# Dense routing weights of an expert layer: one-hot products on TensorE, or 4-byte adds into DRAM by indirect DMA

## The chip, the cores and the metric

The kernel runs on one core of one Trainium2 chip. The metric is the device time of one execution in microseconds (us). Five engines work side by side, each through its own instruction queue in order: PE (TensorE, matrix products), DVE (VectorE), ACT (ScalarE), POOL (GpSimd) and SP (SyncE, which here only issues DMAs). Sixteen DMA engines move data; DMAs are issued from SP, ACT and POOL, and indirect ones, which take their row addresses from a table, from POOL only.

## The reference, cut to what matters

The program is a two-layer backbone (512 latent tokens, 256 context tokens, width 1024). Each layer ends in a product-key expert layer, and the change lies there:

```
q = (hb @ w_q).reshape(n, PEER_HEADS, 2, PEER_DK_HALF)
s = jnp.einsum('nhpk,pek->nhpe', q, keys)
v_top, i_top = lax.top_k(s, PEER_TOPK)
...
e = i1 * N_KEYS + i2
g = jax.nn.softmax(sc.astype(jnp.float32), axis=-1).astype(hb.dtype)
a = jax.nn.gelu(jnp.einsum('nhkd,nd->nhk', u_tab[e], hb)) * g
return jnp.einsum('nhk,nhkd->nd', a, v_tab[e])
```

Each token picks 16 experts in each of 8 heads, 128 slots in all, out of 16,384 experts. An expert is one row of `u_tab` and one of `v_tab`. Two heads of a token may pick the same expert; within a head the 16 are different.

## The kernel before, in words

The latent tokens are four blocks of 128. Block 3 is done sparsely: for each of its 128 slots an indirect DMA gathers the 128 tokens' rows of `u_tab`, DVE takes the dot product (line L907), and the same is done with `v_tab` (L925). Blocks 0 to 2 (384 tokens) are done densely: for each group of 128 experts (an "s block", 128 of them) PE computes all 384 x 128 products `s`, ACT applies the gelu, DVE multiplies by a table of weights that is zero where a token did not pick an expert, and PE adds the product with the 128 rows of `v_tab` to accumulators (L1160).

The function `peer_lat` runs this once per layer in two stages.

1. *Routing stage.* `routing` computes the top-16 lists on DVE, first for block 3 and then for 0, 1 and 2. For a dense block `use` calls `weights_dense`, which builds the table of weights: for four tokens at a time DVE makes two one-hot arrays (L1072, L1075), PE multiplies them (L1079), ACT copies the result (L1081), and one SP DMA per 32 tokens writes 2 MB to the DRAM tensor `gd` (L1083). Between these steps s blocks are computed ahead of need and stored in the DRAM tensor `sp`: 76 in the first layer, 80 in the second.
2. *Dense stage.* `dense` goes over all 128 s blocks. It reads the weights from `gd` (tile `gr`, L1125) and the stored s blocks from `sp` (tile `gsr`), computes those that were not stored, multiplies, splits into a high and a low part, and accumulates. Three blocks are prepared ahead (`AHEAD`).

The order of the instructions on each engine is fixed when the program is built. `Background` objects hold work that is woven in: `tick(us)` is called after a piece of foreground work with its assumed length, and a background object issues as many steps as its rate allows (`rows_bg` the gathers, `s_bg` the s blocks). In `dense` the remaining gathers are spread evenly over the loop. In the first layer the gathers for the context tokens (`gat<-in_peer_v,ev`, with a PE product at L1020) also run in the routing stage. All POOL DMAs use eight semaphores in turn, so that an indirect DMA waits for the landing of the one eight places ahead of it.

Of the kernel before, what the change touches and what calls it, by code (L numbers as in the profile page):

```python
# [11 lines left out]
F32 = mybir.dt.float32  # L12
# [10 lines left out]
SEQ = 512  # L23
# [30 lines left out]
LAG = 3  # L54
COST_T = (2.0, 4.0)
GB = 5
UB, ULAG, VLAG = 3, 2, 1
GTB, VRB, GRB, GSB = 2, 2, 2, 2
AB, AHEAD = 3, 3


def build(nc, tc, I, out):
# [118 lines left out]

    rows_bg, s_bg, ada_bg, conv_bg = (Background() for _ in range(4))

    def tick(us):
        if not any(bg.busy for bg in (rows_bg, s_bg, ada_bg, conv_bg)):
            for bg in (rows_bg, s_bg, ada_bg, conv_bg):
                bg.tick(us)
# [23 lines left out]
    iota = const("iota", [128, 128])  # L211
    rowstart = const("rowstart", [128, 16])
    ones = mk(pc, [128, 128], F32, "ones")
    V.memset(ones, 1.0)
# [828 lines left out]

    def weights_dense(i12, gw, b, gd):


        ps = psum("sm")
        PE.transpose(ps[:, :128], i12[:, 0, :], ident)
        PE.transpose(ps[:, 128:256], i12[:, 1, :], ident)
        PE.transpose(ps[:, 256:384], gw, ident)  # L1050
        it = mk(ph[1], [128, 4, 128], F32, "itT", 1)
        V.tensor_copy(it[:, 0, :], ps[:, :128])
        V.tensor_copy(it[:, 3, :], ps[:, 256:384])
        ei = mk(ph[1], [128, 2, 128], I32, "ik")
        V.tensor_copy(ei[:, 1, :], ps[:, 128:256])
        V.tensor_scalar(ei[:, 0, :], ei[:, 1, :], 4, None, op0=ALU.logical_shift_right)
        V.tensor_scalar(ei[:, 1, :], ei[:, 1, :], 15, None, op0=ALU.bitwise_and)
        V.tensor_copy(it[:, 1:3, :], ei)
        i128 = iota.unsqueeze(1).to_broadcast([128, 4, 128])
        for tq in range(4):  # L1060
            T32 = slice(32 * tq, 32 * tq + 32)
            bc = lambda i, n: it[:, i, T32].unsqueeze(2).to_broadcast([128, 32, n])
            o8 = mk(ph[1], [128, 32, 8], F32, "o8", 1)
            V.tensor_tensor(o8, iota[:, :8].unsqueeze(1).to_broadcast([128, 32, 8]), bc(1, 8), ALU.is_equal)
            V.tensor_tensor(o8, o8, bc(3, 8), ALU.mult)
            o16 = mk(ph[1], [128, 32, 16], F32, "o16", 1)
            V.tensor_tensor(o16, iota[:, :16].unsqueeze(1).to_broadcast([128, 32, 16]), bc(2, 16), ALU.is_equal)
            gt = mk(ph[1], [128, 128, 32], F32, "gt", GTB)
            for t4 in range(8):
                t = slice(4 * t4, 4 * t4 + 4)  # L1070
                o1 = mk(pt, [128, 4, 128], F32, "rstd")
                V.tensor_tensor(o1, i128, it[:, 0, 32 * tq + 4 * t4:32 * tq + 4 * t4 + 4].unsqueeze(2)  # L1072
                                .to_broadcast([128, 4, 128]), ALU.is_equal)
                o2 = mk(pt, [128, 4, 8, 16], F32, "tA")
                V.tensor_tensor(o2, o8[:, t, :].unsqueeze(3).to_broadcast([128, 4, 8, 16]),  # L1075
                                o16[:, t, :].unsqueeze(2).to_broadcast([128, 4, 8, 16]), ALU.mult)
                ps = psum("sm")
                for i in range(4):
# [27 lines left out]
    def dense(l, h, gd, sp, nsp, nb, x, mod):  # L1106
# [13 lines left out]
        def prepare(gi, ei, held={}):  # L1120

            eb = 4 * gi + ei
            if ei == 0:
                held["g"] = gt = mk(ph[1], [128, 4 * nb, 4, 32], F32, "gr", GRB)
                nc.sync.dma_start(gt.rearrange("p b i t -> p b (i t)"),  # L1125
                                  gd.rearrange("b p x -> p b x")[:, 0:4 * nb, 128 * gi:128 * gi + 128])
            if gi < nsp // 4:
# [7 lines left out]
            g3 = gs.rearrange("p (b t) -> p b t", t=32)  # L1135
            V.tensor_tensor(g3, g3, held["g"][:, :, ei, :], ALU.mult)
            ah = mk(ph[1], [128, T], F32R, "ah", AB)
# [43 lines left out]
    def peer_lat(l, C, mod, first=()):  # L1181
# [3 lines left out]
        with psum_pool(s=2):  # L1185
            with psum_pool(**banks), spool("sp", 1) as sp_pool[0]:
                for v in first:
                    g = rows_bg.add(v, 64, V_COST)
                h = norm_mod(xl[0], SEQ, mod, 0, C["norm2_g"], 3)
                gd = mk(pd, [4 * ND, 128, 128 * 32], F32, "gd")  # L1190
# [11 lines left out]
                s_bg.rate, rows_bg.rate = 0.0, rate  # L1202
# [85 lines left out]
    with psum_pool(mm=3, sm=3, acc=2):  # L1288
# [3 lines left out]
        with spool("cxa", 1) as cxa:  # L1292
# [3 lines left out]
            ag = [third(0, g, mod) for g in range(3)]  # L1296
            ada_bg.finish(ag[0])
            mixer_consts(0, C, cm)
            use_bufs(cx, cx, CTX)
# [48 lines left out]
            s_bg.finish()  # L1348
            ada_bg.finish()
            after[0] = None  # L1350
            cx_cm.__exit__(None, None, None)
# [28 lines left out]
    with psum_pool(mm=3, sm=3, acc=2):  # L1380
# [8 lines left out]
        with spool("zx", 1) as zx:  # L1389
# [4 lines left out]
            with spool("ym", 1) as ym:  # L1394
# [6 lines left out]
                with spool("mp", 1) as mp:  # L1401
                    proj = mlstm_proj(1, C, hl, SEQ, True, mp)
                    rows_bg.finish()
                    for i in range(4):
                        add_ctx(xc, i, ond[i], mod_c)
                    close_right(pg_cm)
                    side[0] = "right"
                    use_bufs(zx, None, CTX)
# [8 lines left out]
        cm_cm.__exit__(None, None, None)  # L1417
        px = lat_tail(1, yp, mod)
    pg_cm, pg[0] = right_pool("pg")
    peer_lat(1, C, mod)  # L1420
# [14 lines left out]
def shape_constants():  # L1435
# [17 lines left out]
    c["iota"] = np.tile(np.arange(128, dtype=f), (128, 1))  # L1453
    c["rowstart"] = np.tile(np.array([min(v, 42) for v in STARTS] + [0] * 8, f), (128, 1))
    n_freq = D // 4
# [77 lines left out]
```

## Time and profile before

| | us |
|---|---|
| three runs, median | 4629.89 |
| lowest, highest | 4601.46, 4631.63 |
| the profiled execution | 4608.01 |
| its span, first to last instruction | 4606.2 |

Over the span PE is busy 92%, DVE 72%, ACT 35% and POOL 28%; the 16 DMA engines move 1187 MB, a mean of 258 GB/s. These shares are means over unlike stages. The stretches that matter here are the routing and the dense stage of either layer: about 1337 to 1855 and 1855 to 2610 us in the first, 3392 to 3852 and 3852 to 4580 us in the second.

### The profile page before, as it was taken

The page shows a single profiled execution, that of the slowest core. Times are in us where ns is not written, and L with a number is a line of the kernel's source. Part 1 is how long each engine was busy: PE and PEld are TensorE (multiplying, and loading weights), DVE is VectorE, ACT ScalarE, POOL GpSimd, SP SyncE. Part 2 cuts the span into 40 slices and gives each one's busy share as a digit, 9 for nine tenths or more (in the row PEclk, how much of TensorE's full clock was granted, in tenths as well). Part 3 has the DMA queues.
Part 4 walks back from the last instruction along what each step waited for, and adds up shares of the span by engine and source line. Part 5 has one row for each costly group of instructions (what it writes and reads, how often), then busy time and mean ns, then how long its engine had stood idle before and what let it go on. Part 6 is the DMA issues. An engine that isn't in the chain of part 4 may idle for free.

```text
span 4606.2 us, 61297 instructions
## 1 busy us (share of the span) xinstructions
PE 4250.9 (92%) x22364; PEld 3462.3 (75%) x22364; DVE 3322.1 (72%) x6764; ACT 1631.4 (35%) x2316; POOL 1294.3 (28%) x1061
## 2 busy tenths in 40 slices
PE   7899759987999999999999888999999999999998
PEld 4695545665667799788888764677789998888887
DVE  4754877866578497777777775365699997777775
ACT  4441222323224355333333321243335554333333
POOL 0000345653233341333334344200012322233231
PEclk9999868998999999999999999979999999999999
DMA  8556768986577896999989787512248889899984
GB/s 286 188 153 223 257 211 312 339 296 202 184 260 250 309 347 239 343 332 326 325 316 335 246 284 253 193 56 73 88 138 298 315 295 319 308 313 306 318 311 161
DMA packets 417342, 1187.42 MB, mean 258 GB/s; under 512 B 39440, under 2 KB 142608, under 8 KB 413968
## 3 DMA queue, kind: packets, MB, share of 16 engines
q1 hardware_dynamic: 260992, 631.52, 40.1%
q0 software_dynamic: 150928, 549.52, 33.6%
q8 instruction: 176, 2.88, 0.2%
q10 hardware_dynamic: 5120, 2.47, 0.2%
q14 instruction: 126, 1.03, 0.1%
HBM read 1092.40 MB, written 90.96 MB: 257 GB/s over the span
## 4 chain that ended last, share of the span: by engine, by line
PE 41%; issue 22%; DMA 14%; DVE 10%; POOL 6%; ACT 2%; ACTq 0%; POOLq 0%; DVEq 0%; SPq 0%
PE mm L312 13%; PE s L312 11%; PE acc L1160 9%; POOL gat L876 4%; DMA gsr<-sp 3%; DMA gat<-in_peer_v,ev 3%; DMA vr<-in_peer_v 3%; POOL ug L876 2%; DMA ug<-in_peer_u,hu 2%; PE sm L1079 2%; DMA gat<-in_peer_v,eu 2%; DVE wl L293 1%; PE mm L778 1%; DMA gat<-in_peer_u,eu 1%; DVE vl L293 1%
## 5 line engine op out<-in xcount | busy, mean ns | idle before, releaser
L292 ACT CAST wh<-wr 128x1024 fp32r<-128x1024 f32 x498 | 521.7, 1048 | 1197.8 <-PE mm L312 688.3
L293 DVE TENSOR_TENSOR wl<-wr,wh 128x1024 fp32r<-128x1024 f32 x498 | 606.8, 1219 | 345.1 <-ACT wh L292 339.9
L312 PE MATMUL s<-hh,wh 128*128 128x384 f32 x2048 | 703.1, 343 | 3.0 <-ACT gs L1103 3.0
L312 PE MATMUL s<-hh,wl 128*128 128x384 f32 x2048 | 695.6, 340 | 4.7 <-DVE wl L293 4.7
L312 PE MATMUL s<-hl,wh 128*128 128x384 f32 x2048 | 694.6, 339 | 0.0
L876 POOL DMA_INDIRECT gat<-in_peer_u,eu x256 | 334.1, 1305 | 1265.6 <-DVE pu L820 478.4
L312 PE MATMUL mm<-hh,wl 128*128 128x512 f32 (+1 forms) x1552 | 582.2, 376 | 37.4 <-DVE wl L293 37.3
L1160 PE MATMUL acc<-vh,al 128*128 128x512 f32 x1536 | 604.2, 393 | 13.4 <-DVE al L293 13.1
L1160 PE MATMUL acc<-vl,ah 128*128 128x512 f32 x1536 | 603.1, 393 | 7.5 <-DVE vl L293 7.5
L1160 PE MATMUL acc<-vh,ah 128*128 128x512 f32 x1536 | 601.2, 393 | 9.2 <-ACT vh L292 6.7
L312 PE MATMUL mm<-hh,wh 128*128 128x512 f32 (+1 forms) x1552 | 585.6, 380 | 19.5 <-ACT wh L292 7.8
L312 PE MATMUL mm<-hl,wh 128*128 128x512 f32 (+1 forms) x1552 | 580.3, 375 | 3.6 <-DVE hl L293 2.3
L876 POOL DMA_INDIRECT gat<-in_peer_v,eu x256 | 333.2, 1302 | 642.0 <-PE acc L1160 480.6
L292 ACT CAST vh<-vr 128x1024 fp32r<-128x1024 f32 x256 | 268.7, 1050 | 526.7 <-DMA vr<-in_peer_v 509.8
L876 POOL DMA_INDIRECT gat<-in_peer_v,ev x256 | 296.5, 1158 | 478.5 <-PE acc L1020 350.5
L312 PEld LDWEIGHTS s<-hh,wh 128*128 128x128 f32 x2048 | 387.3, 189 | 29.3 <-issue 14.1
L312 PEld LDWEIGHTS mm<-hh,wh 128*128 128x128 f32 x1552 | 300.7, 194 | 123.0 <-issue 38.1
L312 PEld LDWEIGHTS s<-hh,wl 128*128 128x128 f32 x2048 | 386.7, 189 | 5.7 <-DVE wl L293 5.6
L925 DVE SCALAR_TENSOR_TENSOR hn<-gat,a,hn 128x1024 f32<-128x1024 f32 x254 | 325.2, 1280 | 91.0 <-DMA gat<-in_peer_v,eu 90.4
L312 PEld LDWEIGHTS s<-hl,wh 128*128 128x128 f32 x2048 | 387.4, 189 | 4.4 <-issue 0.8
L312 PEld LDWEIGHTS mm<-hh,wl 128*128 128x128 f32 x1552 | 300.8, 194 | 117.3 <-DVE wl L293 44.0
L293 DVE TENSOR_TENSOR vl<-vr,vh 128x1024 fp32r<-128x1024 f32 x256 | 312.6, 1222 | 79.1 <-ACT vh L292 78.4
(378 smaller groups left out, 7032.4 us busy)
## 6 DMA issues: line engine op xcount, KB each, us to landing
wr<-in_peer_uT SPq DMA_DIRECT2D x256, 512.0 KB
vr<-in_peer_v SPq DMA_DIRECT2D x256, 512.0 KB
wr<-in_w_inT SPq DMA_DIRECT2D x134, 512.0 KB
wada<-in_w_adaT SPq DMA_DIRECT2D x96, 512.0 KB
gd<-gt SPq DMA_DIRECT2D x24, 2048.0 KB
gr<-gd SPq DMA_DIRECT2D x64, 768.0 KB
sp<-gs SPq DMA_DIRECT2D x78, 384.0 KB
gsr<-sp SPq DMA_DIRECT2D x78, 384.0 KB
```

What stands on the lines that cost most here:

```text
L292: S.copy(hi, src)
L293: V.tensor_tensor(lo, src, hi, ALU.subtract)
L312: PE.matmul(ps, w[k][a], x[k][b], start=first and k == 0 and i == 0, stop=last and k == n - 1 and i == 2)
L778: after[0] = PE.matmul(ps[:, :T], w[:, k, :], h[k][0], start=k == 0, stop=k == KT - 1)
L876: d = G.indirect_dma_start(out=t, out_offset=None, in_=tab, in_offset=bass.IndirectOffsetOnAxis(ap=ix, axis=0))
L925: V.scalar_tensor_tensor(on, t, a[:, i:i + 1], on, op0=ALU.mult, op1=ALU.add)
L1079: PE.matmul(ps[:, 128 * i:128 * i + 128], o2[:, i].rearrange("p a b -> p (a b)"), o1[:, i, :], start=True, stop=True)
L1160: mm = PE.matmul(acc[b][half], a[p][:, ts], v[q][:, ds], start=done == 0 and n == 0, stop=done == 127 and n == 2)
```

## The change: what it does

`weights_dense` goes. The table lies in DRAM as `[128 second keys, 128 first keys, 384 tokens]`, one per layer, and is filled with zeros early by 16 DMAs from ACT's queue (first layer: while the context is mixed at the start; second layer: while the context is mixed again). DVE computes for each dense block the flat address of each slot and token (`sx`). For each of a block's 128 slots one indirect DMA from POOL then adds 128 weights, 4 bytes each, into the table: 384 such DMAs per layer. The 16 slots of a head may run side by side; the first of the next head waits until those of the head before have landed, since two heads may name the same expert. The first read of the table waits for the last slots of all blocks. The routing order is now 0, 1, 2, 3, and 112 s blocks are stored ahead in both layers.

```diff
-P0 = (0.4, 0.35, 76)
-P1 = (0.4, 0.35, 80)
+P0 = (0.5, 0.35, 112)
+P1 = (0.3, 0.35, 112)
+S_US = 4.3
+SC_RATE = 1.1
+ZC = (8.0, 12.0)
...
+TL = 128 * ND
+ZN, ZR = 384, 8
...
-    def weights_dense(i12, gw, b, gd):
...
-                V.tensor_tensor(o1, i128, it[:, 0, 32 * tq + 4 * t4:32 * tq + 4 * t4 + 4].unsqueeze(2)
-                                .to_broadcast([128, 4, 128]), ALU.is_equal)
...
-                    PE.matmul(ps[:, 128 * i:128 * i + 128], o2[:, i].rearrange("p a b -> p (a b)"), o1[:, i, :],
-                              start=True, stop=True)
-                S.copy(gt[:, :, t].rearrange("p i t -> p t i"), ps.rearrange("p (t i) -> p t i", t=4))
-                tick(1.4)
-            nc.sync.dma_start(gd[4 * b + tq], gt.rearrange("p i t -> p (i t)"))
+    def zeros(g, p):
...
+        for i in range(n):
+            g.zero.append(nc.scalar.dma_start(dst[i], zt.unsqueeze(1).to_broadcast([128, ZR, ZN])))
+            yield
...
+        def scatter(self, b, i12, gw):
+            ef = mk(pt, [128, 128], F32, "tB")
+            V.scalar_tensor_tensor(ef, i12[:, 1, :], 128.0, i12[:, 0, :], op0=ALU.mult, op1=ALU.add)
+            sx = mk(sp_pool[0], [128, 128], I32, "sx", ND)
+            V.tensor_scalar(sx, ef, float(TL), pos[:, b:b + 1], op0=ALU.mult, op1=ALU.add)
+
+            def steps():
+                before = self.zero
+                for hd in range(8):
+                    now = []
+                    for j in range(16 * hd, 16 * hd + 16):
+                        d = G.indirect_dma_start(out=self.flat, out_offset=bass.IndirectOffsetOnAxis(ap=sx[:, j:j + 1], axis=0),
+                                                 in_=gw[:, j:j + 1], in_offset=None, compute_op=ALU.add)
+                        for p in before:
+                            tc.add_manual_dep(d.ins, p.ins.name, SYNC, reason="the same expert in another head")
...
+                    before = now
+                self.last += before
+            return steps()
...
-                held["g"] = gt = mk(ph[1], [128, 4 * nb, 4, 32], F32, "gr", GRB)
-                nc.sync.dma_start(gt.rearrange("p b i t -> p b (i t)"),
-                                  gd.rearrange("b p x -> p b x")[:, 0:4 * nb, 128 * gi:128 * gi + 128])
+                held["g"] = gt = mk(ph[1], [128, 4, T], F32, "gr", GRB)
+                d = nc.sync.dma_start(gt, gd.w[:, 4 * gi:4 * gi + 4, :])
+                for p in gd.last:
+                    tc.add_manual_dep(d.ins, p.ins.name, SYNC, reason="all slots added")
...
-                        weights_dense(i12, gw, b, gd)
+                        sc_bg.add(gd.scatter(b, i12, gw), 128)
...
-                routing(l, C, h, SEQ, list(range(ND, 4)) + list(range(ND)), use)
-                s_bg.finish()
+                zero_bg.finish()
+                routing(l, C, h, SEQ, list(range(ND)) + list(range(ND, 4)), use)
+                s_bg.rate = 0.0
+                while s_bg.q:
+                    s_bg.step()
+                    tick(S_US)
+                sc_bg.finish()
```

The order of POOL's instructions where the second layer's routing begins, in the kernel before (`gat<-in_peer_u,eu` are block 3's gathers, each with the semaphores that it waits for):

```order
L1036 DMA gat_23425<-ond_3582 128x512 [waits DMASW5_49,DMASW0_49,DVE_49]
L876 DMA gat_26946<-in_peer_u,eu_26900 128x1024 [waits DMASW0_49,DVE_49,DMASW4_49,PE_49,Activation_49]
L876 DMA gat_27023<-in_peer_u,eu_26900 128x1024 [waits DMAHW3_49,DMAHW5_49,DMAHW2_49,DMAHW7_49,DMAHW1_49,DMASW6_49]
L876 DMA gat_27025<-in_peer_u,eu_26900 128x1024
L876 DMA gat_27118<-in_peer_u,eu_26900 128x1024 [waits DMASW7_49]
```

The same place in the changed kernel (`gd<-gw,sx` are the scatters of a block's slots, by block, with their number; waits left off):

```order
L1042 DMA gat_22797<-ond_3603 128x512
L1083 DMA gd_22835<-gw_26056,sx_26302 6291456x1 x64
L1083 DMA gd_22835<-gw_26430,sx_26693 6291456x1 x4
L1083 DMA gd_22835<-gw_26056,sx_26302 6291456x1 x16
...
L1083 DMA gd_22835<-gw_26430,sx_26693 6291456x1 x16
L1083 DMA gd_22835<-gw_26821,sx_27084 6291456x1 x4
...
L882 DMA gat_27546<-in_peer_u,eu_27475 128x1024
```

Where 128 gathers of block 3 stood, the scatters of block 0 and many of block 1 now come first. From the first to the last scatter POOL issues 564 DMAs in the first layer (384 scatters, 40 context gathers, 140 gathers of block 3) and 469 in the second (384 and 85). Gathers that are left after the last scatter: 116 in the first layer, 171 in the second.

SP's order where the dense stage of the first layer begins, in the changed kernel (`wr` loads for s blocks, then the first read of the table):

```order
L1110 DMA wr_18781<-in_peer_uT 128x1024 [waits DMAHW2_49,DVE_49]
L1138 DMA gr_15593<-gd_216 128x1536 [waits DMASW5_49,DMASW6_49,DMASW4_49,DMASW7_49,DMASW3_49,DMAHW1_49,DMASW2_49,DMAHW4_49,DMASW1_49,DMASW0_49]
L1144 DMA gsr_15595<-sp_8999 128x768
L1154 DMA vr_15602<-in_peer_v 128x1024
L1154 DMA vr_15613<-in_peer_v 128x1024 [waits DMAHW3_49]
```

The read of the table waits for all eight of POOL's DMA semaphores (DMASW0 to 7), and every load of the dense stage stands behind it on the same queue.

## Rows read from the trace of the kernel before

**Rows 1.** The page, part 1: busy time and share of each engine.

```profile
span 4606.2 us, 61297 instructions
PE 4250.9 (92%) x22364; PEld 3462.3 (75%) x22364; DVE 3322.1 (72%) x6764; ACT 1631.4 (35%) x2316; POOL 1294.3 (28%) x1061
```

**Rows 2.** Busy time by stretch: routing and dense of each layer, then two shorter.

```profile
core 0: us, PE busy (x) PEld busy (x) DVE busy (x) ACT busy (x) POOL busy (x), PEclk, DMA share, GB/s
1337.00:1855.00 518.00, 491.44 (x3036) 439.30 (x3028) 390.13 (x883) 227.71 (x281) 157.85 (x124) 0.97 0.79 286
1855.00:2600.00 745.00, 728.50 (x3418) 631.78 (x3419) 578.82 (x722) 254.15 (x355) 267.98 (x210) 0.99 0.92 325
3392.00:3852.00 460.00, 449.60 (x2814) 444.70 (x2812) 434.20 (x974) 234.78 (x288) 117.21 (x84) 0.99 0.80 284
3852.00:4580.00 728.00, 716.76 (x3381) 620.97 (x3382) 530.15 (x640) 248.76 (x348) 221.05 (x172) 1.00 0.87 299
3480.00:3600.00 120.00, 119.11 (x769) 117.74 (x768) 119.54 (x258) 66.68 (x79) 35.62 (x25) 1.00 0.84 300
...
200.00:400.00 200.00, 178.86 (x1292) 155.56 (x1290) 115.81 (x263) 81.50 (x133) 1.81 (x2) 0.94 0.53 169
```

**Rows 3.** Waits, 1337 to 1850 us: total, times, longest.

```profile
ACT wh L292 <- PE s L312: 194.0, 64, 11.4
```

**Rows 4.** Timeline of PE: start, length; one-hot products, s blocks, accumulation.

```profile
1762.75 1.05 PE L1079 MATMUL sm<-rstd,tA 128*128 128x128 f32 x8
1763.55 0.42 PE L312 MATMUL s<-hh,wl 128*128 128x384 f32 x1
...
1765.06 0.34 PE L312 MATMUL s<-hh,wl 128*128 128x384 f32 x1
1765.24 0.34 PE L312 MATMUL s<-hh,wh 128*128 128x384 f32 x1
...
4568.51 0.39 PE L1160 MATMUL acc<-vh,ah 128*128 128x512 f32 x1
4568.74 0.39 PE L1160 MATMUL acc<-vl,ah 128*128 128x512 f32 x1
```

**Rows 5.** Line L1160 (accumulation) and L1125 (reads of the table): count, ns, first and last start.

```profile
L1160 PE MATMUL acc<-vh,ah x768: 387/389/628, 1856.9 to 2609.2; 128*128 128x512 f32 x192
...
L1160 PE MATMUL acc<-vh,al x1536: 387/389/795, 1859.2 to 4579.8; 128*128 128x512 f32 x192
...
L1125 SPq DMA_DIRECT2D gr<-gd x64: 377/377/568, 1846.7 to 4506.5; - x64
```

**Rows 6.** Timeline of POOL, 1367 us: start, length, idle before, what ended it.

```profile
1367.02 0.59 POOL L1027 DMA_DIRECT2D ond<-gat  x1 [4.74 <-ACT gat L1026]
1367.92 0.96 POOL L876 DMA_INDIRECT gat<-in_peer_v,ev  x1 [0.30 <-issue]
1369.18 0.94 POOL L876 DMA_INDIRECT gat<-in_peer_v,ev  x1 [0.30 <-issue]
1370.42 0.93 POOL L876 DMA_INDIRECT gat<-in_peer_v,ev  x1 [0.30 <-issue]
```

**Rows 7.** Where a block's indices are ready (`eu`), and one later context gather.

```profile
L889 DVE TENSOR_SCALAR eu<-tB x2: 219/220/220, 1384.3 to 3435.0; 128x128 int32<-128x128 f32 x2
...
1477.32 0.94 POOL L876 DMA_INDIRECT gat<-in_peer_v,ev  x1 [7.72 <-PE acc L1020]
1478.56 0.94 POOL L876 DMA_INDIRECT gat<-in_peer_v,ev  x1 [0.31 <-issue]
```

**Rows 8.** Timelines of POOL and DVE: the second layer's first gather and its use.

```profile
3436.08 0.99 POOL L876 DMA_INDIRECT gat<-in_peer_u,eu  x1 [478.40 <-DVE pu L820]
...
3441.53 1.21 DVE L907 SCALAR_TENSOR_TENSOR gat<-gat,hn 128x1024 f32<-128x1024 f32 x1
```

**Rows 9.** DMA view: GB/s in 40 slices, and sizes by line.

```profile
GB/s 286 188 153 223 257 211 312 339 296 202 184 260 250 309 347 239 343 332 326 325 316 335 246 284 253 193 56 73 88 138 298 315 295 319 308 313 306 318 311 161
...
wr<-in_peer_uT SPq DMA_DIRECT2D x256, 512.0 KB
vr<-in_peer_v SPq DMA_DIRECT2D x256, 512.0 KB
...
gd<-gt SPq DMA_DIRECT2D x24, 2048.0 KB
gr<-gd SPq DMA_DIRECT2D x64, 768.0 KB
...
gsr<-sp SPq DMA_DIRECT2D x78, 384.0 KB
```

More of the change, by code (lines that the diff above doesn't have):

```diff
@@ L55 @@
 COST_T = (2.0, 4.0)
+TL = 128 * ND
+ZN, ZR = 384, 8
 GB = 5
 UB, ULAG, VLAG = 3, 2, 1
-GTB, VRB, GRB, GSB = 2, 2, 2, 2
+VRB, GRB, GSB = 2, 2, 2
 AB, AHEAD = 3, 3
@@ L180, in weave @@
                 yield
-    rows_bg, s_bg, ada_bg, conv_bg = (Background() for _ in range(4))
+    BG = rows_bg, s_bg, ada_bg, conv_bg, sc_bg, zero_bg = [Background() for _ in range(6)]
     def tick(us):
-        if not any(bg.busy for bg in (rows_bg, s_bg, ada_bg, conv_bg)):
-            for bg in (rows_bg, s_bg, ada_bg, conv_bg):
+        if not any(bg.busy for bg in BG):
+            for bg in BG:
                 bg.tick(us)
@@ L212, in build @@
     rowstart = const("rowstart", [128, 16])
+    pos = const("pos", [128, 4])
     ones = mk(pc, [128, 128], F32, "ones")
@@ new lines, in zeros, with __init__ @@
+    def zeros(g, p):
+        zt = mk(p, [128, ZN], F32, "zt")
+        V.memset(zt, 0.0)
+        n = 128 * TL // (ZN * ZR)
+        dst = g.w.rearrange("p e t -> p (e t)").rearrange("p (n r c) -> n p r c", r=ZR, c=ZN)
+        for i in range(n):
+            g.zero.append(nc.scalar.dma_start(dst[i], zt.unsqueeze(1).to_broadcast([128, ZR, ZN])))
+            yield
+    class Weights:
+        def __init__(self, l, p):
+            self.key = "w%d" % l
+            self.w = mk(pd, [128, 128, TL], F32, "gd", 2)
+            self.flat = self.w.rearrange("p e t -> (p e t)").unsqueeze(1)
+            self.zero, self.last = [], []
+            zero_bg.add(zeros(self, p), 128 * TL // (ZN * ZR), ZC[l])
+        def scatter(self, b, i12, gw):
[12 more added lines that the diff above has]
+                            tc.add_manual_dep(d.ins, p.ins.name, SYNC, reason="the same expert in another head")
+                        tc.declare_no_dep(d.ins, group=self.key, keep=[p.ins for p in before],
+                                          reason="other experts or positions")
+                        tc.add_to_no_dep_group(self.key, d.ins)
+                        now.append(d)
+                        yield
+                    before = now
+                self.last += before
+            return steps()
@@ L1085, in s_steps @@
+    gws = []
     def s_steps(l, h, T, sp, n):
@@ L1134, in prepare @@
                 s_block(l, h, T, eb, gs)
[L1135 to L1136 removed]
+            V.tensor_tensor(gs, gs, held["g"][:, ei, :], ALU.mult)
             ah = mk(ph[1], [128, T], F32R, "ah", AB)
@@ L1189, in peer_lat @@
                 h = norm_mod(xl[0], SEQ, mod, 0, C["norm2_g"], 3)
-                gd = mk(pd, [4 * ND, 128, 128 * 32], F32, "gd")
+                gd = gws[l]
                 sp = mk(pd, [max(1, nsp // 4), 128, 4 * T], F32, "sp")
@@ L1198, in use @@
                     else:
-                        weights_dense(i12, gw, b, gd)
+                        sc_bg.add(gd.scatter(b, i12, gw), 128)
                 s_bg.add(s_steps(l, h, T, sp, nsp), nsp)
-                s_bg.rate, rows_bg.rate = 0.0, rate
+                s_bg.rate, rows_bg.rate, sc_bg.rate = 0.0, rate, SC_RATE
                 s_rate[0] = srate
-                routing(l, C, h, SEQ, list(range(ND, 4)) + list(range(ND)), use)
-                s_bg.finish()
+                zero_bg.finish()
[5 more added lines that the diff above has]
+                sc_bg.finish()
                 if first:
@@ L1297, in build @@
             ada_bg.finish(ag[0])
+            gws.append(Weights(0, cxa))
+            zero_bg.rate = 1.0
             mixer_consts(0, C, cm)
@@ L1349, in build @@
             ada_bg.finish()
+            zero_bg.finish()
             after[0] = None
@@ L1406, in build @@
                     close_right(pg_cm)
+                    zt_cm, zp = right_pool("zt")
+                    gws.append(Weights(1, zp))
                     side[0] = "right"
@@ L1418, in build @@
         px = lat_tail(1, yp, mod)
+    zero_bg.finish()
+    close_right(zt_cm)
     pg_cm, pg[0] = right_pool("pg")
@@ L1453, in shape_constants @@
     c["iota"] = np.tile(np.arange(128, dtype=f), (128, 1))
+    c["pos"] = (np.arange(128)[:, None] + 128 * np.arange(4)[None, :]).astype(f)
     c["rowstart"] = np.tile(np.array([min(v, 42) for v in STARTS] + [0] * 8, f), (128, 1))
```

30 lines of the change are left out of this document (removed).

## Prediction

> **What bounds the kernel now.** I read four views. The shares of the page say that PE is busy 92% of the span, and POOL, which gets the new work, 28% [rows 1]. These are means, so the second view is the busy time by stretch: in both routing stages and both dense stages PE is busy 95 to 98% of the time, POOL 25 to 36% [rows 2]. The third is the waits of the first routing stage: ACT waits 194 us for PE's s blocks, not the other way round [rows 3]. The fourth is PE's timeline, which gives the unit costs: an s matmul follows the last after 0.174 us, so an s block (24 of them) takes 4.17 us; an accumulating matmul after 0.2275 us on average, so a block's 18 take 4.10 us; four tokens of one-hot products take 0.80 us and delay their neighbours by some 0.1, say 0.9 us [rows 4]. These account for the stages: the first dense stage computes 52 s blocks and 128 accumulations, 52 x 4.17 + 128 x 4.10 = 742 us, and runs from 1857 to 2610, 753 us [rows 5], so 11 us are start-up. The first routing stage holds 79 s blocks (three are prepared for the dense stage), 330 us, 96 one-hot steps, 86 us, and 102 us of its 518 us [rows 2] remain for the context products and stalls. In the second the 83 s blocks and 96 steps take 346 + 86 of 460 us, and 28 remain. DMA has little to spare in the dense stages: busy 0.92 and 0.87 at 325 and 299 GB/s [rows 2].
>
> **What goes.** 86 us of PE per layer. The one-hot work of DVE and ACT was beside PE; its removal is worth nothing by itself.
>
> **What moves.** 36 s blocks of the first layer and 32 of the second go from the dense to the routing stage: 150 and 133 us change sides, at no cost to PE. The dense stage has 16 s blocks left: 16 x 4.17 + 128 x 4.10 = 592 us, with start-up 603 us. It must be fed. In the second layer it loads 128 blocks of `vr` and 16 of `wr` (0.524 MB each), the table (32 reads of 0.786 MB), 56 pairs of stored blocks (0.393 MB) and 171 gathered tiles (0.524 MB): 75.5 + 25.2 + 22.0 + 89.7 = 212 MB [rows 9]. In 603 us that is 352 GB/s, more than any slice reached (347); at 335, a rate that several slices come near [rows 9], it takes 632 us. The first layer has 116 gathers left, 184 MB, 304 GB/s: PE's 603 us hold there.
>
> **What is added on POOL.** POOL can issue gathers back to back every 1.24 us (0.94 busy, 0.30 between) [rows 6]. With DVE 99% busy a gather took 35.62 / 25 = 1.42, a turn of 1.72 us [rows 2]. No row has a scatter of 4-byte elements with an add. Its nearest rows are the gathers, which also have 128 rows and a table of addresses; only a plain DMA is cheaper, 0.59 + 0.30 = 0.89 us [rows 6]. I bound a scatter's turn by 0.89 and 1.72 and take 1.35, near the uncontended gather, since DVE loses the one-hot work. For gathers between scatters I take 1.35 too.
>
> A head's first scatter waits for the landing of the head before. A gather that starts at 3436.08 is used by DVE at 3441.53 [rows 8], 5.45 us, so up to 4.2 us more than a turn, 24 times per layer. Part is covered by gathers or by another block's scatters put between; I charge 2.5 us each in the second layer (60 us), where few gathers stand between, and 40 us in the first. The Trainium skill (DMA: Bandwidth & Descriptors, Anatomy of one DMA — SWDGE (gpsimd) path) gives a fixed 2.0 us per DMA plus its bytes; by it a wait would exceed a turn by under 0.8 us and both charges together would be 38 instead of 100 us. The row is longer; a 512 KB gather is not a 512 byte scatter, so this stays open by that much.
>
> *First layer.* The first block's indices are ready at about 1384; 152 context gathers stand ahead of the first scatter, and the 152nd went out at about 1478 [rows 7]. I start at 1430. 564 turns x 1.35 = 761, + 40 of waits, + 10 from the first table read to the first accumulation (1846.7 to 1856.9 [rows 5]): 2241. PE has 112 s blocks and the 102 us: 1337 + 467 + 102 = 1906, so it waits for POOL. Dense to 2241 + 603 = 2844, against 2610: **+234**.
>
> *Second layer.* Start 3436 [rows 8]; 469 x 1.35 = 633, + 60 + 10: 4139. PE is done at 3392 + 467 + 28 = 3887. Dense to 4139 + 632 = 4771, against 4580 [rows 5]: **+191**.
>
> *Zeros.* 25 MB per layer. The first layer's are written where DMA is 0.53 busy at 169 GB/s [rows 2] and PE waits for weights now and then: 10 us, bounds 0 and 40. The second layer's fall where slices run at 56 to 138 GB/s [rows 9]: nothing. ACT issues 16 DMAs per layer; ACT is 41% busy there [rows 2]: nothing. The two DVE operations per block for the addresses: nothing, in place of far more.
>
> **Sum.** 234 + 191 + 10 = +435. The profiled execution took 4608 us, 22 below the median of the runs; 4608 + 435 = 5043, say **5040**. At 0.89 us a scatter: first layer 384 x 0.89 + 180 x 1.35 + 50 from 1430 gives 2065, dense to 2668, +58; second 342 + 115 + 70 from 3436 gives 3963, to 4595, +15; with the zeros 4690. At 1.72 for every turn: +445 and +367, 5430.
>
> **The rivals.**
>
> *PE stays the bound (faster).* If a scatter's turn is so short that POOL is done when PE is: dense starts at 1906 + 10 and 3887 + 10, and ends at 2519 and 4529, -91 and -51, with the zeros 4476; without the limit of DMA in the second layer 4450. It needs a turn of (1906 - 1430 - 40 - 243) / 384 = 0.50 us in the first layer and (3887 - 3436 - 60 - 115) / 384 = 0.72 us in the second. From the low bound each 0.1 us is worth 77 us, so the sign changes at 0.79 us. For: 4 bytes instead of 4 KB move per row, and PE's share makes any relief of PE count. Against: POOL's 0.94 us is the same for every uncontended gather, and even a plain DMA takes 0.89. Chance 22%.
>
> *The add makes a scatter twice as long.* If the read of the old value needs as much issuing as a gather of its own, a turn is 1.24 + 0.94 = 2.18 us: first layer 837 + 243 + 50 from 1430, to 3163; second 837 + 115 + 70 from 3436, to 5090: +553 and +510, 5680. Landing could do the same: eight semaphores in turn let a DMA wait for the eighth before it, so a landing above 8 x 1.35 = 10.8 us would set the turn. No row shows an add. Chance 13%.
>
> *The turn lies between 0.73 and 1.0 us.* 4560 to 4770, where the gain on PE and the loss on POOL nearly cancel. Chance 14%, 6 of them within 1% of the time before.
>
> That the change is not carried out can be excluded by the order: the 768 scatters stand on POOL, and the one-hot products are gone.
>
> **How the numbers follow.** The forecast, POOL's turns as the bound with 1.0 to 1.72 us, has 51%: 4770 to 5430, likeliest 5040. 1% is about what a measurement of this kernel can tell from no change. Faster by over 1%: 22%; within: 6%; slower: 72%, the 51, 13 and 8 of the third rival. The range leaves out half of the faster cases, below 4480, and most of the doubled add, above 5550: 4480 to 5550.
>
> **What would show it.** In the profile after, POOL should be busy 75% or more of both routing stages, these should last some 800 us (first) and 745 us (second) against 518 and 460, with PE idle for the last 250 to 330 us of each, and the wait that ends it should be the table read's for POOL's DMAs. A scatter's row should read 0.95 to 1.4 us, with stops of a few us every 16 of them. The dense stages should take 603 and 632 us. I am wrong if the scatter's row is under half a microsecond, if PE is 95% busy in the routing stages, or if POOL stands idle for long between scatters, waiting for landings.

## The result, and the profile after

The changed kernel takes 5676.7 us (median of 4 runs, 5671.0 to 5680.7) against 4616.0 for the kernel before beside it: ratio 1.2305, interval 1.2277 to 1.2334. The direction was forecast, the size was not: 5040 us, at most 5550. By stage, from the first and last starts of the lines that bound each (us):

| | before | forecast | after |
|---|---|---|---|
| first s matmul, first layer | 1337.7 | 1337 | 1398.4 |
| routing stage, first layer | 519 | 904 | 1129 |
| dense stage, first layer | 753 | 603 | 616 |
| between the layers | 783 | 783 | 793 |
| routing stage, second layer | 460 | 747 | 1069 |
| dense stage, second layer | 728 | 632 | 637 |

The dense stages came as forecast; nearly all of the miss is in the routing stages. The first and last accumulations (all, then the second layer's) give the bounds of the dense stages:

```profile
L1173 PE MATMUL acc<-vh,ah x1536: 387/389/793, 2527.0 to 5642.1; 128*128 128x512 f32 x192
...
L1173 PE MATMUL acc<-vh,ah x768: 387/389/632, 5005.5 to 5642.1; 128*128 128x512 f32 x192
```

The page's first part, to be laid beside [rows 1]:

```profile
span 5669.2 us, 58527 instructions
...
PE 4308.5 (76%) x20810; PEld 3443.8 (61%) x20810; DVE 3068.7 (54%) x6286; ACT 1439.8 (25%) x2123; POOL 2534.4 (45%) x1829
```

The busy time by stretch, columns as in [rows 2]: routing and dense of each layer, then the first 200 us.

```profile
1390.00:2520.00 1130.00, 690.89 (x3110) 605.11 (x3108) 419.08 (x886) 184.21 (x258) 892.82 (x598) 0.79 0.67 172
2520.00:3130.00 610.00, 576.28 (x2543) 476.28 (x2544) 429.66 (x512) 205.84 (x282) 134.33 (x112) 0.98 0.83 296
4000.00:4960.00 960.00, 452.72 (x2205) 439.02 (x2204) 294.28 (x528) 138.29 (x190) 749.96 (x481) 0.73 0.55 128
4960.00:5640.00 680.00, 638.90 (x2861) 532.54 (x2860) 478.96 (x579) 218.58 (x304) 201.44 (x150) 0.98 0.83 301
0.00:200.00 200.00, 137.76 (x752) 81.06 (x752) 68.71 (x186) 52.47 (x95) 5.65 (x13) 0.83 0.92 344
```

In the routing stages PE's busy share fell from 95 and 98% to 61 and 47%, POOL's rose to 79 and 78%. The group of the scatters by line: count, ns (lowest, median, highest), first and last start; then what ended POOL's idle time before them, in us and times, and how long their landing took.

```profile
L1083 POOL DMA_INDIRECT gd<-gw,sx x768: 1538/1553/2636, 1455.7 to 4879.9; - x192
...
  issue: 229.2, 724
  DMA gd<-gw,sx: 23.6, 23
...
DMA to landing us min/median/max: 2.9/3.4/9.1
```

A scatter holds POOL for 1.55 us at the median (1.54 at least) where a gather held it 0.94 [rows 6]; 0.30 us lie between two, as between gathers. The stops for landings, for which the forecast charged 100 us, come to 24 in all. POOL's timeline where the second layer's scatters begin, as [rows 8] showed the first gather there, and one of the longer stops for a landing:

```profile
3980.39 1.64 POOL L1083 DMA_INDIRECT gd<-gw,sx  x1 [485.13 <-ACT hn L902]
3982.34 1.57 POOL L1083 DMA_INDIRECT gd<-gw,sx  x1 [0.30 <-issue]
...
4016.51 1.54 POOL L1083 DMA_INDIRECT gd<-gw,sx  x1 [1.70 <-DMA gd<-gw,sx]
```

Before PE computes an s block, ACT and DVE split its tile `wr` into a high part `wh` and a low part `wl` (L298, L299); "split" means this below. The waits from 3930 to 5010 us show a second thing (total, times, longest):

```profile
DVE gat L913 <- DMA gat<-in_peer_u,eu: 647.1, 71, 255.2
...
PE s L318 <- DVE wl L299: 510.5, 42, 251.3
```

DVE waits for a gather of block 3 once for 255 us, PE for a split by DVE as long. The last scatter ends at 4881.8, yet the first accumulation starts at 5005.5: PE was still computing s blocks.

**The budget of the miss.** The first accumulation of the first layer came 286 us later than forecast: the scatters took 1055 us from first to last instead of 801 (+254), started 26 late, and 6 are left. The second layer's routing stage is 322 us longer than forecast: scatters 901 instead of 693 us (+208), and 124 instead of 10 from the last scatter to the first accumulation (+114). With 13 and 5 in the dense stages and 10 between, less the 10 us for the zeros that the forecast had charged elsewhere, that is 626; 5043 + 626 = 5669, against 5671 us for the profiled execution.

### The profile page after: what moved, and what is told of

It reads as the page before. It is cut to its first block, busy times and chain, and to the rows that moved or that the text cites. A ratio compares the mean times of both kernels' runs of the same rounds, so it can differ in the third digit from the quotient of the medians.

```text
span 5669.2 us, 58527 instructions
## 1 busy us (share of the span) xinstructions
PE 4308.5 (76%) x20810; PEld 3443.8 (61%) x20810; DVE 3068.7 (54%) x6286; ACT 1439.8 (25%) x2123; POOL 2534.4 (45%) x1829
## 5 line engine op out<-in xcount | busy, mean ns | idle before, releaser
L1083 POOL DMA_INDIRECT gd<-gw,sx x768 | 1311.2, 1707 | 744.1 <-ACT hn L902 485.1
L318 PE MATMUL s<-hh,wl 128*128 128x384 f32 x2048 | 777.8, 380 | 836.1 <-DVE wl L299 836.0
L298 ACT CAST wh<-wr 128x1024 fp32r<-128x1024 f32 x498 | 521.1, 1048 | 2491.2 <-PE s L318 1653.8
L318 PEld LDWEIGHTS s<-hh,wl 128*128 128x128 f32 x2048 | 443.0, 216 | 876.1 <-DVE wl L299 868.2
L913 DVE SCALAR_TENSOR_TENSOR gat<-gat,hn 128x1024 f32<-128x1024 f32 x256 | 312.7, 1225 | 1180.0 <-DMA gat<-in_peer_u,eu 1176.0
L299 DVE TENSOR_TENSOR wl<-wr,wh 128x1024 fp32r<-128x1024 f32 x498 | 607.3, 1222 | 413.9 <-ACT wh L298 411.9
L318 PE MATMUL s<-hh,wh 128*128 128x384 f32 x2048 | 762.3, 372 | 8.5 <-ACT gs L1116 8.5
L318 PE MATMUL s<-hl,wh 128*128 128x384 f32 x2048 | 755.6, 369 | 0.0
L318 PEld LDWEIGHTS s<-hh,wh 128*128 128x128 f32 x2048 | 442.8, 216 | 33.6 <-issue 16.2
L318 PEld LDWEIGHTS s<-hl,wh 128*128 128x128 f32 x2048 | 439.5, 215 | 9.6 <-issue 8.4
L298 ACT CAST vh<-vr 128x1024 fp32r<-128x1024 f32 x256 | 269.1, 1051 | 680.3 <-DMA vr<-in_peer_v 666.3
L882 POOL DMA_INDIRECT ug<-in_peer_u,hu x192 | 226.4, 1179 | 386.3 <-DVE ug L992 172.4
L882 POOL DMA_INDIRECT gat<-in_peer_u,eu x256 | 285.5, 1115 | 228.2 <-PE acc L1173 126.0
```

The source lines that it names most:

```text
L298: S.copy(hi, src)
L299: V.tensor_tensor(lo, src, hi, ALU.subtract)
L318: PE.matmul(ps, w[k][a], x[k][b], start=first and k == 0 and i == 0, stop=last and k == n - 1 and i == 2)
L882: d = G.indirect_dma_start(out=t, out_offset=None, in_=tab, in_offset=bass.IndirectOffsetOnAxis(ap=ix, axis=0))
L913: V.scalar_tensor_tensor(t, t, 1.0, hn, op0=ALU.mult, op1=ALU.mult, accum_out=a[:, i:i + 1])
L1083: d = G.indirect_dma_start(out=self.flat, out_offset=bass.IndirectOffsetOnAxis(ap=sx[:, j:j + 1], axis=0), in_=gw[:, j:j + 1], in_offset=N ...
```

## The experiments

Theory: a scatter with add costs POOL a turn of about 2.0 us, and gathers behind scatters stop DVE, and through it PE. Rivals: landings, PE, the zeros or DMA set the stages.

**Without the add.** The scatter writes instead of adding.

```diff
-in_=gw[:, j:j + 1], in_offset=None, compute_op=ALU.add)
+in_=gw[:, j:j + 1], in_offset=None)
```

> The scatters write their 128 values instead of adding them; all else, number, order and waits, as in the changed kernel. Theory A (the add makes the issue longer: POOL writes out a second read per element): POOL's scatter falls from 1.55 to about 0.94 us, a turn from 2.0 to about 1.3 us, 768 x 0.65 = 500 us less: about 5170 us. Theory B (the length is that of a scatter to 128 single addresses in DRAM, add or not): 1.55 us stays, about 5670 us. Theory C (the landing of the adds holds POOL back through the eight semaphores): the scatter's own row stays at 1.55 and the gaps between shrink, which are 0.30 us already: no more than 30 us less.

5237.0 us, ratio 1.1352 (1.1312 to 1.1391). The scatters' line:

```profile
L1083 POOL DMA_INDIRECT gd<-gw,sx x768: 954/961/2340, 1460.4 to 4443.8; - x192
```

The row falls by 0.59 us at the median; 768 x 0.59 = 453, measured 440 (500 expected). A scatter without add holds POOL about as long as a gather does. The single 4-byte targets are not the price; the add is. Why the add takes longer is not shown.

**Half of the slots.** Heads 0 to 3 alone are scattered.

```diff
-                for hd in range(8):
+                for hd in range(4):
...
-                        sc_bg.add(gd.scatter(b, i12, gw), 128)
+                        sc_bg.add(gd.scatter(b, i12, gw), 64)
```

> Only heads 0 to 3 are scattered (384 instead of 768 DMAs; the weights of the other four heads are left out). If POOL's turns bound both routing stages: 384 x 2.0 = 770 us less, about 4910 us, a little more than that if PE becomes the bound in the second layer. If the time is lost elsewhere (zeros, table reads, DMA share), far less than 400 us.

5117.1 us, ratio 1.1092 (1.1044 to 1.1139), 207 more than expected. The scatters end after 532 and 444 us, but the first accumulation follows 278 and 312 us later. The window before the end of the second layer's scatters:

```profile
3880.00:4125.00 245.00, 71.82 (x350) 68.74 (x351) 55.77 (x79) 20.12 (x28) 196.30 (x130) 0.65 0.47 114
```

And the longest of DVE's waits from 3640 to 4125 us:

```profile
DVE gat L913 <- DMA gat<-in_peer_u,eu: 279.7, 20, 233.5
```

PE worked 72 of 245 us while s blocks were still to do. POOL alone does not set the stage: DVE, and PE behind it, wait for gathers.

**No gathers woven in between, second layer.** The rate of block 3's gathers is zero in the routing stage.

```diff
-P1 = (0.3, 0.35, 112)
+P1 = (0.0, 0.35, 112)
```

> In the second layer no gather of block 3 is woven into the routing stage (rate 0 instead of 0.3); all 256 run in the dense stage. Theory D (DVE stands in line before a gather that POOL issues late, and the s blocks behind it on DVE and PE are late too): the scatters end at 384 x 2.0 = 770 us after the first instead of 901, PE has its s blocks done by then, the 125 us from the last scatter to the first accumulation shrink to about 15, and the dense stage grows from 637 to about 767 us (257 MB at 335 GB/s): 5677 - 131 - 110 + 130 = about 5565 us. Without theory D (PE is late for a reason of its own) the 125 us stay: about 5675 us.

5581.4 us, ratio 1.2098 (1.2053 to 1.2143), near the 5565 expected, but 98 us instead of 15 still pass between the last scatter and the first accumulation. Four gathers still stand among the scatters on POOL (4540 to 4576 us). What waiting for the first of them does, first in a window:

```profile
4200.00:4450.00 250.00, 0.00 (x0) 0.00 (x0) 0.00 (x0) 0.00 (x0) 208.52 (x136) 0.50 0.23 0
```

Then DVE's wait from 4000 to 4860 us:

```profile
DVE gat L913 <- DMA gat<-in_peer_u,eu: 432.5, 3, 403.4
```

For these 250 us nothing runs but POOL.

**The zeros at another rate.** The steps of the zeros in the first layer are charged 32 instead of 8 us.

```diff
-ZC = (8.0, 12.0)
+ZC = (32.0, 12.0)
```

> The first layer's zeros are written at a quarter of the pace (one DMA per 32 us of foreground work instead of 8). In the changed kernel everything after the first 200 us stands 52 us later than before, with DMA 92% busy in those 200 us. If the zeros in front of the first weight loads cause that: 30 to 50 us less, about 5635 us. If the shift has another cause: within 10 us of 5677.

5669.5 us, ratio 1.2286 (1.2255 to 1.2318). It tells nothing of the zeros: the 16 DMAs were issued from 17 to 164 us, as without the edit (17 to 162).

**Gathers last, both layers.** Block 3's gathers are handed over after the last scatter.

```diff
-                        rows_bg.add(u_rows(), 128)
-                        rows_bg.add(v_rows(xl[0]), 128)
+                        late.extend([u_rows(), v_rows(xl[0])])
...
                 sc_bg.finish()
+                for v in late:
+                    rows_bg.add(v, 128)
```

> Block 3's gathers are put on POOL behind the last scatter, in both layers; all else as in the changed kernel. Theory (a scatter holds POOL for a turn of about 2.0 us; the 125 us between the last scatter and the first accumulation of the second layer come from DVE's order, in which dot products that wait for late gathers stand in front of the splits that feed PE's s blocks): the second layer's scatters run back to back, 384 x 2.0 = 768 us, and the first accumulation follows the last scatter within 15 us instead of 125; routing about 1070 - 245 = 825 us in the second layer and about 890 in the first. The dense stages then load 256 gathered tiles each, 257 MB, 770 us at 335 GB/s instead of 616 and 637. In all about 5440 us. Rival (POOL's sum of work alone sets the stages): 140 and 85 gathers fewer at 1.3 us, the tail of 125 us stays, the dense stages lengthen alike: about 5610 us.

5472.5 us, ratio 1.1875 (1.1842 to 1.1908), near the 5440, yet 64 and 103 us remain between last scatter and first accumulation. DVE's timeline of the second layer shows why:

```profile
4029.15 1.23 DVE L299 TENSOR_TENSOR wl<-wr,wh 128x1024 fp32r<-128x1024 f32 x1 [2.93 <-ACT wh L298]
4429.84 1.22 DVE L913 SCALAR_TENSOR_TENSOR gat<-gat,hn 128x1024 f32<-128x1024 f32 x1 [399.46 <-DMA gat<-in_peer_u,eu]
...
4433.74 2.36 DVE L299 TENSOR_TENSOR wl<-wr,wh 128x1024 fp32r<-128x1024 f32 x2
```

A dot product stood in DVE's queue between two splits, and its gather stood behind hundreds of scatters on POOL (it was issued at 4426 us, the first scatter at 3871): 399 us without a split.

**No scatters.** The table stays zero.

```diff
-                for hd in range(8):
+                for hd in range(0):
```

> No scatter is issued, the table stays zero (the slots' additions are left out); the zeros, the stored s blocks and the order of routing stay. Theory (scatters alone make the loss, about 600 us a layer): PE is the bound again in the routing stages, about 530 and 480 us, dense 616 and 637, the start 52 us late: about 4530 us. Rival (the new order of routing, with block 3's gathers late, stalls DVE and PE by itself): routing stages of 650 us or more and a total over 4750.

4655.6 us, ratio 1.0091 (1.0062 to 1.012): neither 4530 nor 4750. The scatters make 1021 of the change's 1061 us. But the rest of the change, without the one-hot work, with 112 stored blocks and with the zeros, gains nothing either: routing 639 and 554 us, dense 597 and 634, and the first s matmul stands 71 us later than in the kernel before. PE's largest wait in the first routing stage (1409 to 2048 us) is again one for DVE:

```profile
PE s L318 <- DVE wl L299: 56.3, 41, 3.4
```

**Zeros late.** The first layer's zeros are issued after the context's recurrent mixer, each after a modulation product.

```diff
+            if not gws[1:]:
+                tc.add_manual_dep(g.zero[-1].ins, ada_mm[0].ins.name, SYNC, reason="leave the memory to the loads before")
...
-            gws.append(Weights(0, cxa))
-            zero_bg.rate = 1.0
...
+            gws.append(Weights(0, cxa))
+            zero_bg.rate = 1.0
```

> The first layer's 16 zero DMAs are issued after the context's recurrent mixer instead of in the first 160 us, and each waits for the modulation product issued last. Theory (the zeros hold up the loads of the modulation weights at the start, where DMA is 0.99 and 0.86 busy): the first context gather moves from 556 to about 515 us, the total falls by 30 to 50 us, to about 5635. Rival (25 MB cost the same 50 us wherever they are written, or the delay has another cause): 5665 to 5690.

5634.3 us, ratio 1.2232 (1.2195 to 1.227), as expected 42 less. The first context gather moves from 556 to 532 us (515 expected), against 504 before: by this mark the zeros cost some 50 us where they were, and half of that where they are now (111 to 262 us). Of the 42 us 22 are gained up to the first s matmul; the other 20 are spread over later stages, which the edit does not touch.

**The kernel before with 112 stored s blocks.**

```diff
-P0 = (0.4, 0.35, 76)
-P1 = (0.4, 0.35, 80)
+P0 = (0.4, 0.35, 112)
+P1 = (0.4, 0.35, 112)
```

> The kernel before with 112 stored s blocks in either layer instead of 76 and 80, nothing else. Theory (moving s blocks from the dense to the routing stage is free, PE being the bound of both): within 15 us of the kernel before, routing longer by 150 and 133 us and dense shorter by as much. Rival (the stored blocks' way through DRAM, or the block gathers that find less room, cost more): slower by 30 us or more.

4766.1 us, ratio 1.0327 (1.029 to 1.0364): the rival's side, slower by 30 us or more. Routing grew by 144 and 133 us, near the price; dense shrank by 63 and 63 only. A window of the first dense stage:

```profile
2070.00:2680.00 610.00, 542.34 (x2302) 439.53 (x2302) 482.37 (x612) 181.52 (x251) 269.22 (x191) 0.96 0.95 339
```

What ACT waits for in it, and in the first dense stage of the kernel before (1850 to 2590 us):

```profile
ACT vh L292 <- DMA vr<-in_peer_v: 373.9, 99, 10.9
...
ACT vh L292 <- DMA vr<-in_peer_v: 261.5, 63, 10.9
```

DMA is 0.95 busy at 339 GB/s, and ACT waits 374 us for `vr` where it waited 262 in a longer window: with fewer s blocks this dense stage is held up by its loads. What is moved into the routing stage costs there in full, and less than half is given back.

**Gathers gated.** As gathers last, and each gather that goes before the dense loop's own pacing waits for the last stored s block.

```diff
-        S.activation(out, ps[:, :T], AF.Gelu_apprx_tanh)
+        last_s[0] = S.activation(out, ps[:, :T], AF.Gelu_apprx_tanh)
...
-            gate[0] = pace[-3] if len(pace) > 2 else None
+            gate[0] = pace[-3] if len(pace) > 2 else gate[0]
...
+                gate[0] = last_s[0]
```

> As the run with block 3's gathers last, but each early gather also waits for the last stored s block. There four gathers of the second layer had still been placed ahead of 288 scatters' end; their dot product stood in DVE's queue and stopped the splits for 399 us, PE with them. Theory (one late gather in DVE's queue is what keeps PE from the s blocks): now all s blocks are done while POOL scatters, the first accumulation follows the last scatter within 15 us instead of 64 and 103; 5472 - 50 - 90 = about 5330 us. Rival (the tail has another cause, for instance PE or the loads of wr held back by the scatters' own traffic): s blocks still run after the last scatter, 5430 us or more.

5347.4 us, ratio 1.1595 (1.1566 to 1.1624), the 5330 of the theory; the first accumulation follows the last scatter by 17 us in both layers. Two windows of the second layer's scatters:

```profile
3950.00:4100.00 150.00, 150.00 (x868) 150.00 (x867) 44.18 (x36) 51.73 (x72) 128.04 (x73) 1.00 0.70 174
4300.00:4600.00 300.00, 0.00 (x0) 0.00 (x0) 0.00 (x0) 0.00 (x0) 243.21 (x158) 0.50 0.22 0
```

PE does its s blocks without a gap beside the scatters, is done before 4300 and stands for 300 us while POOL goes on. The scatters, alone on POOL, run from 3834.3 to 4607.3: 773 / 384 = 2.01 us a turn. This is the scatter's price with nothing else on POOL.

**No scatters, 76 and 80 stored.**

```diff
-P0 = (0.5, 0.35, 112)
-P1 = (0.3, 0.35, 112)
+P0 = (0.5, 0.35, 76)
+P1 = (0.3, 0.35, 80)
```

(beside the edit of the run without scatters)

> No scatter is issued (the slots' additions are left out) and 76 and 80 s blocks are stored as in the kernel before, so only the one-hot work is gone and the zeros are new. Theory (the one-hot steps cost PE 86 us a layer; storing 112 blocks loses some 75 us a layer since the shortened dense stage then waits for DMA): routing about 450 and 390 us, dense about 750 and 730, start 60 us late: about 4520 us, 135 less than without scatters at 112 stored blocks. Rival (the number of stored blocks does not matter once the one-hot work is gone): within 30 us of 4656.

4536.4 us, ratio 0.9843 (0.9811 to 0.9875), 119 less than with 112. Routing 455 and 392 us, 64 and 68 below the kernel before; the first dense stage is 21 us shorter, the first s matmul stands 62 us later, 9 us are lost between the layers. So with these zeros and this order, leaving the one-hot products out altogether gains about 80 us; a replacement that costs anything gains less.

**One block of three.** The kernel before, with block 0's weights alone scattered, and routed first.

```diff
-                        weights_dense(i12, gw, b, gd)
+                        if b == 0:
+                            sc_bg.add(gws[l].scatter(i12, gw), 128)
+                        else:
+                            weights_dense(i12, gw, b, gd)
...
-                routing(l, C, h, SEQ, list(range(ND, 4)) + list(range(ND)), use)
...
+                routing(l, C, h, SEQ, [0, 3, 1, 2], use)
```

> The kernel before, but block 0's weights of each layer go by 128 scatters with add into a zeroed quarter of the old table; blocks 1 and 2 keep the one-hot products, 76 and 80 stored blocks, block 0 routed first. POOL has room for 128 turns of 2.0 us (256 us) in a routing stage of 430 us or more. Theory (a third of the one-hot work, 29 us a layer, comes off PE and nothing else changes; a third of the zeros costs about 15 us): about 4565 us, ratio 0.99. Rival (block 3's gathers, issued behind or among the scatters, come late and stop DVE and PE as in the changed kernel): 4620 us or more.

4886.1 us, ratio 1.058 (1.0552 to 1.0608). Routing 625 and 583 us, dense 753 and 748 (753 and 728 before). What waits in the first routing stage (1360 to 1990 us), then in the second (3529 to 4112):

```profile
PE acc L1023 <- DMA gat<-in_peer_v,ev: 103.9, 31, 11.0
...
DVE gat L910 <- DMA gat<-in_peer_u,eu: 154.3, 12, 71.8
```

128 scatters fit into POOL's idle time by their sum, and the last one starts 251 and 237 us before the first accumulation; yet the routing stages are 106 and 123 us longer. In the first PE waits 104 us for the context's gathers, in the second DVE waits 154 us for block 3's: gathers stand behind the scatters on POOL. The order of routing changed too, which this run does not part from that.

**Gated, zeros late, without the add.**

```diff
-in_=gw[:, j:j + 1], in_offset=None, compute_op=ALU.add)
+in_=gw[:, j:j + 1], in_offset=None)
```

(beside the edits of the runs gated and zeros late)

> Gathers gated as before, zeros late, and the scatters write without adding (a slot that two heads share keeps one head's weight: the addition is left out). It shows what a scatter with a gather's price would have given with the other two losses removed. Theory: turn 1.36 us, 384 turns 522 us; routing about 660 and 590 us, dense about 690 each; 1376 + 660 + 690 + 788 + 590 + 690 + 27 = about 4820 us, still slower than the kernel before. Rival (PE is the bound as soon as a scatter costs a gather's turn): routing 640 and 555 us, total under 4760.

5527.6 us, ratio 1.1993 (1.1937 to 1.2049): 180 us *more* than gated with the add, which neither side expected. The scatters are done after 585 and 519 us, but 356 and 376 us of s blocks follow. PE's timeline beside the scatters:

```profile
4130.22 0.48 PE L318 MATMUL s<-hl,wh 128*128 128x384 f32 x1 [2.32 <-issue]
4133.02 0.48 PE L318 MATMUL s<-hh,wl 128*128 128x384 f32 x1 [2.32 <-issue]
4135.82 0.48 PE L318 MATMUL s<-hh,wh 128*128 128x384 f32 x1 [2.32 <-issue]
```

One matmul every 2.8 us, and PE waits for nothing that the profile shows. (ACT and DVE often wait there for what the profile calls `remote`, another core or an unknown queue.)

**The same with the zeros where the change has them.**

```diff
-            if not gws[1:]:
-                tc.add_manual_dep(g.zero[-1].ins, ada_mm[0].ins.name, SYNC, reason="leave the memory to the loads before")
...
```

> As the run with gated gathers, the zeros where the change has them, but the scatters write without adding (a slot that two heads share keeps one head's weight). Theory (scatters without add that follow each other every 1.3 us starve the other engines, wherever the zeros are written): the stretch from the last scatter to the first accumulation is over 300 us in both layers, total 5500 to 5600 us. Rival (the late zeros did it): first accumulation within 20 us of the last scatter, total about 4860 us.

5556.3 us, ratio 1.2061 (1.1995 to 1.2128), with 356 and 371 us after the last scatter: not the zeros. The second layer's scatters begin at 3917 us, and at first PE keeps busy beside them:

```profile
3917.00:3957.00 40.00, 35.54 (x197) 35.03 (x195) 36.36 (x136) 13.62 (x20) 29.83 (x25) 0.96 0.45 145
3977.00:4117.00 140.00, 24.91 (x56) 16.47 (x57) 9.68 (x19) 4.35 (x5) 105.64 (x110) 0.50 0.05 11
```

In the first window DVE is still busy with routing, some scatters take longer, and 25 go out in 40 us, one every 1.6 us; in the second they go out every 1.27 us, and PE is busy 25 of 140 us. Here POOL paused once, from 4131 to 4160 us, for nothing that the profile shows; its timeline:

```profile
4130.04 0.96 POOL L1083 DMA_INDIRECT gd<-gw,sx  x1 [0.30 <-issue]
4160.25 0.95 POOL L1083 DMA_INDIRECT gd<-gw,sx  x1 [29.25 <-issue]
```

In that pause PE resumed (its timeline), and ran on nearly without a gap:

```profile
4139.15 0.69 PE L318 MATMUL s<-hh,wh 128*128 128x384 f32 x1 [21.07 <-ACT gs L1116]
4139.63 0.52 PE L318 MATMUL s<-hl,wh 128*128 128x384 f32 x1
```

**The same with a memset on POOL after each scatter.**

```diff
+            fl = mk(sp_pool[0], [128, 512], F32, "fl", 1)
...
+                        G.memset(fl, 0.0)
```

> As the last, with one memset of 128x512 on POOL after each scatter; in the second layer the program's order puts these memsets ahead of all scatters, so only the first layer's scatters are spaced, to a turn of about 2 us. Theory (the rate of issue starves the engines): in the first layer PE is busy beside the scatters and the first accumulation follows the last scatter within 20 us, in the second layer it comes more than 300 us after. Rival (the missing add does it, at any rate): more than 300 us in both layers.

5325.8 us, one run. Of the second layer's 384 memsets 365 are done before its first scatter, and 332 us follow its last one. In the first layer they alternate with the scatters from about 1780 us on (some 20 stand between earlier ones), and 17 us follow. Its windows:

```profile
1640.00:1700.00 60.00, 10.60 (x24) 7.02 (x24) 1.22 (x1) 1.53 (x2) 45.37 (x49) 0.50 0.07 16
1700.00:1780.00 80.00, 14.17 (x31) 9.04 (x31) 1.22 (x1) 1.53 (x2) 59.13 (x70) 0.50 0.04 7
1800.00:1900.00 100.00, 100.00 (x580) 100.00 (x579) 28.20 (x23) 34.14 (x49) 90.58 (x100) 1.00 0.51 170
```

With 49 scatters and no memset in 60 us PE is busy 11; with 53 scatters and 47 memsets in 100 us (a turn of 1.9 us) PE is busy all 100. So the missing add alone does not hold PE up. What the engines lack in the first case is not shown.

## Why the prediction was wrong

- **What bounds the kernel now:** right for the stages' shares. But PE is not the only bound of the dense stage: shortened, it waits for DMA. The forecast used this for the second layer alone.
- **What goes, 86 us of PE a layer:** without scatters and with 76 and 80 stored blocks the routing stages were 64 and 68 us shorter than in the kernel before: three quarters of it.
- **What moves "at no cost to PE":** right for PE, wrong as a price. In the kernel before the move costs 158 us by itself. The forecast's dense stages were still right (616 and 637 against 603 and 632), where 116 and 171 gathers were left (208 in the first dense stage before); in the routing stages the moved blocks were hidden under POOL's turns. The rival in which PE stays the bound, at 4476, was 180 us too low: without scatters the kernel takes 4656. Its dense stages came (597 and 634 us); its routing stages took 60 and 49 us more than the 579 and 505 that its numbers give, with PE waiting 56 and 49 us for DVE's splits, and the first s matmul stood 71 us later, with 10 charged.
- **What is added on POOL, the step that failed:** a scatter's turn was bounded by 0.89 and 1.72 us and taken as 1.35, near the gather. Alone on POOL it is 2.01: 1.54 busy at least, 0.30 between, the rest from slower ones and landings. That is above the upper bound, and the difference, 768 x 0.66 = 507 us, is the larger part of the miss: POOL's stretches from first to last scatter came 462 us longer than forecast, 507 from the scatters and some 30 from the gathers between, less 76 charged too much for landings. The bound was taken from rows without an add; the nearest row had the same table of addresses but not the operation that cost. The rival of a doubled add put the loss where it lay, in the add, at 2.18 us, and gave 5680, close to the measured 5677; that a second read is the reason is not shown. The closeness is partly luck: its turn was 8% too long and its landings 76 us too dear, and it held nothing for DVE's stops.
- **A gather that DVE waits for, missed:** the forecast let gathers among the scatters cost their turn on POOL only. A gather behind scatters is late; its dot product stands in DVE's queue before the splits of the next s blocks; so PE stops, and SP's loads with it. In the second layer this leaves s blocks for 124 us after the last scatter. Gathers that wait until all s blocks are done save 330 us in all, part of it the gathers' own turns, and the tail is gone. The sign that the table's read waits for POOL came in the first layer only (last scatter 2509, read 2512); in the second the read went out at 4996, 114 us after the scatters, behind the last loads for s blocks.
- **Landings:** 24 us measured, 100 charged. A scatter lands after 2.9 us at least, 3.4 at the median, far below the 5.45 us of the 512 KB gather [rows 8]. By the fixed cost of 2.0 us that the Trainium skill gives (DMA: Bandwidth & Descriptors, Anatomy of one DMA — SWDGE (gpsimd) path) the stops are estimated at 38 us. The trace lies above the 2.0 us, yet the rule was the nearer one for 512 bytes.
- **Zeros, 10 us with bounds 0 and 40:** late zeros save 42 us and leave part of the delay; 52 us at the first context gather, or 61 at the first s matmul, is the better number. Not the 0.53 busy stretch took them: they went out from 17 to 162 us, where DMA then reads 0.92 (0.72 before). The second layer's cost at most the 10 us by which the stretch between the layers grew.

## What to carry to other kernels

Price an indirect DMA on POOL by its operation, not by its bytes: if no row shows the operation, the upper bound must hold a second pass of the nearest row. Before putting late work on a queue, list what stands behind its consumer on the in-order engine: a transfer that is late by one queue stops every later instruction of the consumer's engine, and moving it to the end helps in full only if its consumer moves too. Work moved out of a stage is worth only what that stage's next limit, here the loads, leaves of it.

## What the runs showed of the hardware

- An indirect DMA of 128 addresses holds POOL 0.94 us as a gather of 4 KB rows, 0.96 us as a scatter of 4 bytes, and 1.55 us as a scatter of 4 bytes with add (a gather between others, medians for the scatters), with 0.30 us between two.
- Scatters without add that follow each other without a break (turn 1.26 us) slow the other engines to one PE matmul every 2.8 us, with DMA 0.02 to 0.10 busy; adds at 2.0 us, a 0.54 us memset between most scatters (turn 1.9 us), or a turn of 1.6 us while DVE is busy with routing, do not. The granted clock falls to 0.50 there (1.2 of 2.4 GHz), with PE busy 11 of 60 us. That the sequence on POOL does it rests on the memsets and on POOL's own pause; what is short in between, instructions for one, was only thought of, not shown.
